# FFN operands loaded in place, loads of the output projection in another order, one operand made on VectorE

## The chip, the cores and the metric

The kernel runs on one core of a Trainium2 chip. The metric is the device time of one execution in microseconds; before the change it is 3053.76 us, the median of three runs (3052.32 to 3055.01).

## The reference

One layer of a streaming encoder works on 2048 prompt frames and 64 frames of a running stream, 2112 rows of 1024 values. An RMSNorm and an input projection feed two groups of heads: four retention heads (decaying state, group norm, gate) and eight heads of softmax attention with a forget bias. Their outputs stand side by side as `mix`, 1024 columns. What matters here comes after that:

```python
mix = concatenate([ret_output(o_r, g_r, gn_gain), o_f])
x = x + mix @ w_out
h = rmsnorm(x, g_ffn)
x = x + (silu(h @ w_gate) * (h @ w_up)) @ w_down      # width 2816
y = rmsnorm(x, norm_final_gain)
```

All of it is float32. The kernel gets float32 accuracy out of reduced-precision products by cutting every operand into a high part and a low part (`split`, L83: ScalarE copies the source rounded into the high part, VectorE writes source minus high part into the low part) and adding three products, high by high, high by low and low by high.

## The kernel before

TensorE multiplies 128x128 weights with up to 512 columns. All loads and stores are issued from one queue, SP's, in one order. The order on each engine is fixed when the program is built: a planner takes the instructions of the written program, with their costs and their data dependences, and lays them out per engine as early as its own timing allows. So instructions of a later stage can stand ahead of earlier ones where an engine would be idle. At run time nothing is reordered: an instruction that waits holds up all that stands behind it on its engine or queue.

The stages: input projection and attention projections; retention heads interleaved with the attention over the cache and then with the prompt's attention (`f_stream`); the output projection (`p3_stream`, L508); the FFN.

**Output projection.** 17 tiles of 128 rows. `load_m` (L513) brings a tile of `mix` transposed (`m`, 512 KB) and, for the prompt, the reciprocal softmax sums (`rb`, two loads of 128 KB, repeated over partitions). `halves` (L534) multiplies the attention half of `m` by `rb` (L537) and splits it into `mT`. `products` (L589) runs 24 matmuls for each of two column halves (L594); VectorE adds `x`, the residual (L633); `norm` (L544) squares and sums on ScalarE (L91), takes the root on GpSimd (L93, L95), writes the normed `h` on VectorE (L547) and stores the new `x`. `back` (L551) transposes `h` of the tile before by eight TensorE transposes (L557) in two groups that share one PSUM tile, each copied out by ScalarE (L558). It stands in the middle of the next tile's second half. After every second tile `operands` (L567) makes seven combinations of the two tiles' transposes (sums and differences for a seven-product scheme that replaces eight half-size products of the FFN), and stores them to DRAM, `h2_d` (in the trace `h_d`).

Tiles 0 to 6 run beside the prompt's attention; tile 7 and the rest need the last attention results (`f_done`), so that ten tiles run alone. The buffers `raw` of the pool `ws` are two, and `m`, `rb`, `operands`' scratch `t`, the staging of `load_h` and the first FFN weights all take turns in them.

**FFN.** Three blocks of 768, 768 and 576 rows; per block 11 pairs of 128-column stripes of the weights. `load_h` (L1032) brings a block's seven operands from `h2_d` in 14 pieces of 384 KB into staging buffers, and splits each into `hb`, one tile that holds all seven operands, high and low. For block 0 `prefetch` (L1059) does this beside the output projection, a piece at a time as tiles are done. `gu(i, s)` (L1133) runs the seven products of stripe pair `i` for the gate (s = 0) and the up projection (s = 1), 12 matmuls each (L1179); `prep` (L1087) makes and splits their weight operands four products ahead and asks for the next weights (`load_w`, L1051) when it has taken the last one; `down` (L1197) is the down projection. At a block's end L1245 to L1262 load and split the next block's operands, taking turns in two up-weight buffers (`rup`) and two down-weight buffers (`rawd`), beside the down projection; the next up weights are loaded after that (L1262).

Of the kernel before, what the change touches and what calls it, by code (L numbers as in the profile page):

```python
# [9 lines left out]
F32 = mybir.dt.float32  # L10
# [28 lines left out]
def hybrid_kernel(ctx: ExitStack, tc: tile.TileContext, a: dict):  # L39
# [468 lines left out]
    def p3_stream(last):  # L508
# [58 lines left out]
        def operands(j, b1, b2):  # L567

            w = b1.shape[2]
            lo, hi = slice(0, 4), slice(4, 8)  # L570
            t = (p3.tile([128, D], F32, tag="h", name="t", bufs=1).rearrange("p (k t) -> p k t", k=KT) if j == NT // 2 else
                 ws.tile([128, KT, 128], F32, tag="raw", name="t"))[:, :, 0:w]

            def out(n, src):
                dma(h2_d[n, :, :, j * 128:j * 128 + w], src)

            out(0, b1[:, lo])
            out(2, b1[:, hi])
            out(6, b2[:, hi])
            ve.tensor_tensor(t[:, lo], b2[:, lo], b1[:, lo], op=ALU.subtract)  # L580
            ve.tensor_tensor(t[:, hi], b2[:, hi], t[:, lo], op=ALU.subtract)
            ve.tensor_tensor(b2[:, lo], b2[:, hi], b2[:, lo], op=ALU.subtract)
            out(4, t[:, lo])
            out(1, t[:, hi])
            out(3, b2[:, lo])
            ge.tensor_tensor(b1[:, hi], t[:, hi], b1[:, hi], op=ALU.subtract)
            out(5, b1[:, hi])

# [21 lines left out]
        with tc.tile_pool(name="p3", bufs=2, reuse_waits="tile") as p3:  # L610
# [5 lines left out]
            for i in range(NT):  # L616
                while i + 1 < 16 and (i + 1) // 8 not in f_done:
                    yield None
                x = x_t.pop(i)
                if i + 1 < NT:  # L620
                    load_x(i + 1)
                    if i:
                        load_m(i + 1)
                mT = mT_t.pop(i) if i else None
                for c in range(2):
                    for q, ps in enumerate(products(mT, c) if i else early[c:c + 1]):
                        if (c, q) == (1, 1):
                            yield from back(i - 1)
                        if (c, q) == (1, 0) and 0 < i < NT - 1:
                            halves(i + 1)  # L630
                        yield 1300
                    d = slice(c * 512, (c + 1) * 512)
                    ve.tensor_tensor(x[:, d], ps, x[:, d], op=ALU.add)  # L633
# [397 lines left out]

    def load_h(n, raws):  # L1032

        hf = BLOCKS[n][1] // 2
        c0 = BLOCKS[n][0] // 2
        hb = hb_t[n] = hp.tile([128, 7, 2, 4, HALF], F32R, tag="hb", name="hb")
        raw_h = []

        def load(x):
            raw = raws()[:, 0:2 * hf].rearrange("p (k t) -> p k t", k=2)  # L1040
            j, k = divmod(x, 2)
            dma(raw, h2_d[j, :, 2 * k:2 * k + 2, c0:c0 + hf])
            raw_h.append(raw)

        yield load
        for x in range(14):
            j, k = x // 2, x % 2 * 2
            split(hb[:, j, 0, k:k + 2, 0:hf], hb[:, j, 1, k:k + 2, 0:hf], raw_h[x])
            yield None

# [8 lines left out]
    def prefetch():  # L1059

        g = load_h(0, lambda: ws.tile([128, D], F32, tag="raw", name="raw"))
        load = next(g)
        for x in range(14):
            load(x)
            next(g)
            yield 8 + x // 2 if x < 13 else 15
        load_w(0, 0, ws)
        yield 15

# [8 lines left out]
    with tc.tile_pool(name="fw", bufs=1, reuse_waits="tile") as fw, \  # L1078
# [8 lines left out]
        def prep(x):  # L1087
# [20 lines left out]
            split(o[:, 0], o[:, 1], (r0[:, lo], s2, r0[:, hi], r1[:, lo], s1, r1[:, hi], r0[:, hi])[j])  # L1108
            if j == 6 and i + 1 < NB * NP and not (s == 1 and i % NP == NP - 1):
                load_w(i + 1, s, rup if s else ws)  # L1110
# [22 lines left out]
        def gu(i, s):  # L1133

            n = i // NP
            hf = BLOCKS[n][1] // 2
            hb = hb_t[n]
            ps_t = {}
# [30 lines left out]
            for j in range(7):  # L1169
# [7 lines left out]
                for k in range(4):  # L1177
                    for m, (u, v) in enumerate(((0, 0), (0, 1), (1, 0))):
                        te.matmul(ps, w[:, u, k], hb[:, j, v, k, 0:hf], start=b == j and k == 0 and m == 0,  # L1179
                                  stop=j not in (0, 4) and k == 3 and m == 2, skip_group_check=True)  # L1180
# [44 lines left out]
        for i in range(NB * NP):  # L1225
# [13 lines left out]
            for j in gu(i, 1):  # L1239
# [3 lines left out]
                if p == NP - 1 and j in (3, 5):  # L1243
                    split_d(i, j // 4)
            if p == NP - 1 and n + 1 < NB:  # L1245
                ring = [lambda: rup.tile([128, D], F32, tag="raw", name="raw"),
                        lambda: fw.tile([128, D], F32, tag="rawd", name="rawd", bufs=2)]
                pick = [ring[x % 4 // 2] for x in range(14)]
                g = load_h(n + 1, lambda: pick.pop(0)())
                load = next(g)  # L1250
                for x in range(4):
                    load(x)
                todo = down(i)
                for x in range(14):
                    next(g)
                    if x + 4 < 14:
                        load(x + 4)
                    if x % 2 and x > 1:
                        next(todo)
                for _ in todo:  # L1260
                    pass
                load_w(i + 1, 1, rup)  # L1262
            elif p == NP - 1:
# [67 lines left out]
```

## Time and profile before

| | us |
|---|---|
| median of three runs | 3053.76 (3052.32 to 3055.01) |
| the profiled execution, its own time | 3053.89 |
| its span in the trace | 3052.1 |
| TensorE matmul busy | 2940.8 (96%) |
| VectorE busy | 1998.9 (65%) |
| ScalarE busy | 1253.6 (41%) |
| GpSimd busy | 379.4 (12%) |

The profile's second part cuts the span into 40 slices of 76 us, one digit per slice for each engine: its busy share in tenths. A row named PEclk gives the clock that TensorE was granted, in the same tenths of full speed. TensorE's busy time counts a matmul longer when the granted clock is lower, so busy time alone hides such a loss. The output projection alone on the core is at about 1437 to 1606 us of the span, the FFN's blocks begin at about 1603, 2106 and 2613 us.

### The profile page before, as it was taken

What the parts mean: (1) busy time and instruction counts of PE and PEld (TensorE: products, weight loads), DVE (VectorE), ACT (ScalarE), POOL (GpSimd) and SP (SyncE); (2) the same over time, 40 slices, a digit from 0 to 9 for tenths busy, and PEclk for the clock granted to TensorE, in tenths of its full rate; (3) what the DMA queues carried; (4) which work ended last, traced back from release to release, by engine and by line L of the source; (5) the groups of instructions that cost most, each with busy time, mean ns of one, the idle gap of its engine ahead of it and who ended that gap; (6) DMA issues with size and microseconds to landing.
All of it is one profiled execution on the core that took longest, in us unless ns stands there. A gap on an engine that the chain in (4) does not pass through costs nothing. (4 is left out here: it accounts for less than half of the span.)

```text
span 3052.1 us, 44866 instructions
## 1 busy us (share of the span) xinstructions
PE 2940.8 (96%) x16684; PEld 2644.4 (87%) x16684; DVE 1998.9 (65%) x3908; ACT 1253.6 (41%) x2642; POOL 379.4 (12%) x525
## 2 busy tenths in 40 slices
PE   8999899999999999899878999999999999999998
PEld 8999778888888888787658999998999999888887
DVE  4333554476766666765336777778777777888886
ACT  4233333265655555654223333334433333543333
POOL 0000012111111111100001101101101101211111
PEclk9999999999999999999899999999999999999999
DMA  6565533233422222544655221224522221632221
GB/s 196 173 185 174 170 110 96 88 109 89 136 76 64 80 84 86 165 140 123 196 174 168 83 69 56 84 70 131 159 70 59 83 68 58 196 97 83 84 84 59
DMA packets 438812, 341.62 MB, mean 112 GB/s; under 512 B 26954, under 2 KB 388298, under 8 KB 438594
## 3 DMA queue, kind: packets, MB, share of 16 engines
q1 hardware_dynamic: 438594, 338.76, 37.5%
q8 instruction: 131, 2.15, 0.3%
q14 instruction: 87, 0.71, 0.1%
HBM read 253.29 MB, written 85.40 MB: 111 GB/s over the span
## 5 line engine op out<-in xcount | busy, mean ns | idle before, releaser
L1179 PE MATMUL mm<-hb,w 128*128 128x384 f32 (+1 forms) x5544 | 905.6, 324 | 21.8 <-DVE G L1152 13.9
L1179 PEld LDWEIGHTS mm<-hb,w 128*128 128x128 f32 x5544 | 895.3, 189 | 31.2 <-issue 13.1
L1208 PE MATMUL dn<-wd,act 128*128 128x512 f32 (+1 forms) x2244 | 518.3, 390 | 3.1 <-ACT wd L85 3.1
L1208 PEld LDWEIGHTS dn<-wd,act 128*128 128x128 f32 (+1 forms) x2244 | 413.4, 185 | 96.2 <-ACT wd L85 3.3
L492 PE MATMUL mm<-w,hT 128*128 128x512 f32 x1632 | 445.7, 408 | 0.7 <-DVE hT L86 0.5
L1209 DVE TENSOR_TENSOR y<-y,dn 128x512 f32<-128x512 f32 (+1 forms) x374 | 254.8, 685 | 163.3 <-PE dn L1208 163.1
L86 DVE TENSOR_TENSOR w<-raw,w 128x512 fp32r<-128x512 f32 (+1 forms) x358 | 313.2, 888 | 52.2 <-ACT w L85 46.2
L492 PEld LDWEIGHTS mm<-w,hT 128*128 128x128 f32 x1632 | 291.4, 190 | 56.3 <-issue 2.2
L85 ACT CAST w<-raw 128x512 fp32r<-128x512 f32 (+1 forms) x358 | 220.9, 643 | 218.6 <-PE mm L1179 123.2
L232 PE MATMUL mm<-w,hT 128*128 128x386 f32 x1632 | 299.2, 342 | 0.9 <-ACT hT L85 0.9
L232 PEld LDWEIGHTS mm<-w,hT 128*128 128x128 f32 x1632 | 289.2, 190 | 1.6 <-ACT hT L85 1.4
L594 PE MATMUL mm<-w,mT 128*128 128x512 f32 x816 | 221.1, 420 | 14.2 <-ACT mT L85 13.2
L85 ACT CAST wd<-rawd 128x512 fp32r<-128x512 f32 x132 | 75.6, 619 | 381.4 <-PE dn L1208 380.1
L899 ACT ACTIVATE P<-P,nm 128x512 f32<-128x512 f32 (+3 forms) x288 | 189.6, 661 | 90.0 <-DVE nm L893 89.6
L85 ACT CAST hi<-t 128x512 fp32r<-128x512 f32 (+1 forms) x288 | 154.8, 562 | 138.7 <-PE t L916 135.0
L86 DVE TENSOR_TENSOR lo<-t,hi 128x512 fp32r<-128x512 f32 (+1 forms) x288 | 183.0, 656 | 37.9 <-ACT hi L85 36.2
L594 PEld LDWEIGHTS mm<-w,mT 128*128 128x128 f32 x816 | 157.8, 201 | 53.2 <-ACT mT L85 17.5
L1099 POOL TENSOR_TENSOR s<-raw 128x512 f32<-128x512 f32 x33 | 68.6, 2079 | 1058.2 <-DVE w L86 1023.8
L916 PE MATMUL t<-ident,P 128*128 128x128 f32 x1088 | 159.9, 276 | 9.1 <-DVE lo L86 5.5
L932 PE MATMUL pv<-hi,V 128*128 128x256 f32 x576 | 153.4, 292 | 1.6 <-DVE o L941 0.8
L916 PEld LDWEIGHTS t<-ident,P 128*128 128x128 f32 x1088 | 128.0, 142 | 30.2 <-DVE lo L86 10.0
L882 DVE TENSOR_SCALAR_CACHE_REDUCE P<-s 128x512 f32<-128x512 f32 x192 | 129.6, 684 | 30.6 <-PE s L879 26.2
(228 smaller groups left out, 3655.6 us busy)
## 6 DMA issues: line engine op xcount, KB each, us to landing
raw<-w_gate SPq DMA_DIRECT2D x66, 512.0 KB
raw<-w_up SPq DMA_DIRECT2D x66, 512.0 KB
rawd<-w_down SPq DMA_DIRECT2D x66, 512.0 KB
hf<-hT_d SPq DMA_DIRECT2D x34, 512.0 KB
qk_d<-qkT SPq DMA_DIRECT2D x32, 512.0 KB
h_d<-hT SPq DMA_DIRECT2D x40, 256.0 KB
KA<-qk_d SPq DMA_DIRECT2D x72, 128.0 KB
V<-v_d SPq DMA_DIRECT2D x36, 256.0 KB
```

Source lines behind the costliest of these rows:

```text
L85: se.copy(hi, src)
L86: ve.tensor_tensor(lo, src, f32(hi), op=ALU.subtract)
L232: te.matmul(ps, hT[:, u, k], w[:, v, k], start=n == 0, stop=n == 23)
L492: te.matmul(ps, hT[:, u, k], w[:, v, k], start=k == 0 and j == 0, stop=k == 7 and j == 2)
L594: te.matmul(ps, mT[:, u, k], mix_w[4 + c][:, v, k], start=k == 0 and j == 0, stop=k == 7 and j == 2)
L882: ve.tensor_scalar(o, ps, 1.0, None, op0=ALU.mult, op1=ALU.min, accum_out=m)
L899: se.activation(v, v, AF.Exp, bias=nm, scale=-1.0, accum_out=sum_t[h, u // 4][:, i % 8, ch:ch + 1])
L916: te.transpose(tr[:, c * 128:(c + 1) * 128], P_t[n, e, j // 2][:, k * 128:(k + 1) * 128], ident)
L932: te.matmul(o, V, hi[:, p], start=j == 0 and c == 0, stop=False)
L1179: te.matmul(ps, w[:, u, k], hb[:, j, v, k, 0:hf], start=b == j and k == 0 and m == 0, stop=j not in (0, 4) and k == 3 and m == 2, skip_gro ...
L1208: te.matmul(ps, act_t[i][e][:, u, f:f + m], w[c][:, v, e], start=e == 0 and j == 0, stop=e == 1 and j == 2)
L1209: ve.tensor_tensor(y[:, d], y[:, d], ps, op=ALU.add)
```

## The change

Three edits. First, the seven FFN operands are seven tiles `hb0` to `hb6` in place of one, and each is loaded by one transfer straight into the place of its low part; the split then reads that place and overwrites it. The staging buffers drop out. At a block's end the load of operand j is written behind product j of the block's last up projection, the splits stand beside the down projection, and the next up weights are loaded where they are in every other stripe pair. Second, in the output projection `load_m` of the tile after next is written right behind `halves`, and `load_x` in the middle of a tile's first half. `operands`' scratch `t` takes the buffer of `h` for every pair, where before only the last did. Third, the seventh operand is made on VectorE in a tile of its own, `t4`. The first gate weights are asked for when tile 16 is done, before it was tile 15.

```diff
@@ operands
-            t = (p3.tile([128, D], F32, tag="h", name="t", bufs=1).rearrange("p (k t) -> p k t", k=KT) if j == NT // 2 else
-                 ws.tile([128, KT, 128], F32, tag="raw", name="t"))[:, :, 0:w]
+            t = p3.tile([128, D], F32, tag="h", name="t", bufs=1).rearrange("p (k t) -> p k t", k=KT)[:, :, 0:w]
...
-            ge.tensor_tensor(b1[:, hi], t[:, hi], b1[:, hi], op=ALU.subtract)
-            out(5, b1[:, hi])
+            t4 = p3.tile([128, 4, 128], F32, tag="t4", name="t4", bufs=1)[:, :, 0:w]
+            ve.tensor_tensor(t4, t[:, hi], b1[:, hi], op=ALU.subtract)
+            out(5, t4)
 @@ p3_stream
                 x = x_t.pop(i)
-                if i + 1 < NT:
-                    load_x(i + 1)
-                    if i:
-                        load_m(i + 1)
+                if i and i + 1 < NT and i + 1 not in m_t:
+                    load_m(i + 1)
                 mT = mT_t.pop(i) if i else None
                 for c in range(2):
                     for q, ps in enumerate(products(mT, c) if i else early[c:c + 1]):
                         if (c, q) == (1, 1):
                             yield from back(i - 1)
+                        if (c, q) == (0, 2 if i else 0) and i + 1 < NT:
+                            load_x(i + 1)
                         if (c, q) == (1, 0) and 0 < i < NT - 1:
                             halves(i + 1)
+                            if i + 2 == 16 or i + 2 < 16 and (i + 2) // 8 in f_done:
+                                load_m(i + 2)
                         yield 1300
 @@ load_h
+    def load_h(n, j):
+        hf = BLOCKS[n][1] // 2
+        c0 = BLOCKS[n][0] // 2
+        hb = hb_t[n, j] = hp.tile([128, 2, 4, HALF], F32R, tag=f"hb{j}", name="hb")
+        dma(hb[:, 1, :, 0:hf], h2_d[j, :, :, c0:c0 + hf])
+
+    def split_h(n, j):
+        hf = BLOCKS[n][1] // 2
+        hb = hb_t[n, j]
+        for k in (0, 2):
+            split(hb[:, 0, k:k + 2, 0:hf], hb[:, 1, k:k + 2, 0:hf], f32(hb[:, 1, k:k + 2, 0:hf]))
 @@ prefetch
-        for x in range(14):
-            load(x)
-            next(g)
-            yield 8 + x // 2 if x < 13 else 15
+        for j in range(7):
+            load_h(0, j)
+            yield 7 + j
+            split_h(0, j)
+        yield 16
         load_w(0, 0, ws)
-        yield 15
+        yield 99
 @@ prep
-            if j == 6 and i + 1 < NB * NP and not (s == 1 and i % NP == NP - 1):
+            if j == 6 and i + 1 < NB * NP:
                 load_w(i + 1, s, rup if s else ws)
 @@ the loop over stripe pairs
             for j in gu(i, 1):
...
+                if p == NP - 1 and n + 1 < NB:
+                    load_h(n + 1, j)
             if p == NP - 1 and n + 1 < NB:
-                ring = [lambda: rup.tile([128, D], F32, tag="raw", name="raw"),
-                        lambda: fw.tile([128, D], F32, tag="rawd", name="rawd", bufs=2)]
...
-                load_w(i + 1, 1, rup)
+                split_h(n + 1, 0)
+                for j, _ in enumerate(down(i), 1):
+                    split_h(n + 1, j)
```

## Rows read from the trace of the kernel before

**Rows 1.** Part 1 of the page: busy time, share of the span, instructions.

```profile
PE 2940.8 (96%) x16684; PEld 2644.4 (87%) x16684; DVE 1998.9 (65%) x3908; ACT 1253.6 (41%) x2642; POOL 379.4 (12%) x525
```

**Rows 2.** Stretches of the span by engine, with granted clock and DMA share.

```profile
core 0: us, PE busy (x) PEld busy (x) DVE busy (x) ACT busy (x) POOL busy (x), PEclk, DMA share, GB/s
1290.00:1436.70 146.70, 141.09 (x818) 120.62 (x818) 93.91 (x209) 80.17 (x184) 10.49 (x17) 0.98 0.48 132
1436.70:1605.80 169.10, 136.42 (x555) 104.93 (x554) 65.80 (x85) 45.01 (x73) 16.56 (x26) 0.90 0.61 185
1602.80:1632.80 30.00, 19.98 (x89) 17.97 (x88) 16.98 (x27) 11.81 (x20) 6.80 (x7) 0.84 0.99 288
...
2130.00:2170.00 40.00, 33.66 (x188) 32.41 (x187) 36.58 (x54) 20.00 (x39) 14.67 (x14) 0.99 0.89 284
...
2636.00:2680.00 44.00, 37.79 (x240) 35.58 (x239) 38.12 (x62) 21.81 (x45) 15.46 (x15) 0.92 0.78 245
```

**Rows 3.** Waits of TensorE from 1436.7 to 1605.8: total us, times, longest.

```profile
PE rt L557 <- ACT hT L558: 12.5, 4, 4.5
PE mm L594 <- ACT mT L85: 11.9, 7, 3.3
```

**Rows 4.** Timeline: the norm's last step of tiles 6 and 16 (start, us, instruction).

```profile
1436.67 1.29 DVE L547 SCALAR_TENSOR_TENSOR h<-x,r,gffn 128x1024 f32<-128x1024 f32 x1 [1.10 <-POOL r L95]
...
1605.84 1.29 DVE L547 SCALAR_TENSOR_TENSOR h<-x,r,gffn 128x1024 f32<-128x1024 f32 x1 [1.09 <-POOL r L95]
```

**Rows 5.** Timeline: a tile whose sums came late, and `m` of the next.

```profile
1453.92 1.30 SPq L48 DMA_DIRECT2D rb<-rsum_d  x2
...
1462.24 0.69 DVE L537 TENSOR_TENSOR m<-m,rb 128x512 f32<-128x512 f32 x1 [3.47 <-DMA rb<-rsum_d]
...
1463.49 0.58 ACT L558 COPY hT<-rt 128x512 f32<-128x512 f32 x1
...
1464.12 0.66 PE L557 MATMUL rt<-ident,h 128*128 128x128 f32 x4 [1.94 <-ACT hT L558]
...
1464.34 0.38 SPq L48 DMA_DIRECT2D m<-mix_d  x1
...
1468.11 0.62 ACT L85 CAST mT<-m 128x512 fp32r<-128x512 f32 x1 [2.71 <-DMA m<-mix_d]
```

**Rows 6.** Timeline: a tile without a wait of TensorE.

```profile
1493.96 0.60 PE L557 MATMUL rt<-ident,h 128*128 128x128 f32 x4
...
1495.33 0.61 PE L557 MATMUL rt<-ident,h 128*128 128x128 f32 x4
...
1500.94 1.06 ACT L91 ACTIVATE h<-x 128x1024 f32<-128x1024 f32 x1 [2.15 <-issue]
...
1503.02 1.28 DVE L547 SCALAR_TENSOR_TENSOR h<-x,r,gffn 128x1024 f32<-128x1024 f32 x1 [2.17 <-POOL r L95]
...
1506.03 0.60 PE L557 MATMUL rt<-ident,h 128*128 128x128 f32 x4
```

**Rows 7.** Groups of instructions, 1436.7 to 1605.8: busy, mean ns, idle before.

```profile
L86 DVE TENSOR_TENSOR hb<-raw,hb 128x768 fp32r<-128x768 f32 x14 | 13.3, 953 | 11.3 <-ACT hb L85 11.3
...
L586 POOL TENSOR_TENSOR hT<-t,hT 128x512 f32<-128x512 f32 x5 | 8.3, 1662 | 44.3 <-DVE t L581 44.3
```

**Rows 8.** A wait of SP's queue, 1436.7 to 1605.8: total us, times, longest.

```profile
SPq L48 <- DVE mT L86: 16.3, 5, 7.4
```

**Rows 9.** Timeline at the FFN's entry: first products, what waited for weights.

```profile
1602.84 0.51 PE L1179 MATMUL mm<-hb,w 128*128 128x384 f32 x2
...
1611.74 0.62 ACT L85 CAST w<-raw 128x512 fp32r<-128x512 f32 x1 [1.46 <-DMA raw<-w_gate]
...
1624.01 1.31 POOL L1099 TENSOR_TENSOR s<-raw 128x512 f32<-128x512 f32 x1 [10.53 <-DMA raw<-w_up]
```

**Rows 10.** Timeline: first block change, the up weights' load and a late product.

```profile
2124.70 1.24 SPq L48 DMA_DIRECT2D raw<-w_up  x2
...
2169.59 2.90 PE L1179 MATMUL mm<-hb,w 128*128 128x384 f32 x8 [3.44 <-DVE G L1152]
```

More of the change, by code (lines that the diff above doesn't have):

```diff
@@ L1030, in hybrid_kernel @@
     hb_t, raw_t, w_t, sum_t = {}, {}, {}, {}
-    def load_h(n, raws):
+    def load_h(n, j):
         hf = BLOCKS[n][1] // 2
         c0 = BLOCKS[n][0] // 2
[L1036 to L1045, printed above, removed]
-        for x in range(14):
-            j, k = x // 2, x % 2 * 2
-            split(hb[:, j, 0, k:k + 2, 0:hf], hb[:, j, 1, k:k + 2, 0:hf], raw_h[x])
-            yield None
+        hb = hb_t[n, j] = hp.tile([128, 2, 4, HALF], F32R, tag=f"hb{j}", name="hb")
[5 more added lines that the diff above has]
+            split(hb[:, 0, k:k + 2, 0:hf], hb[:, 1, k:k + 2, 0:hf], f32(hb[:, 1, k:k + 2, 0:hf]))
     def load_w(i, s, pool):
@@ L1059, in prefetch @@
     def prefetch():
-        g = load_h(0, lambda: ws.tile([128, D], F32, tag="raw", name="raw"))
-        load = next(g)
-        for x in range(14):
-            load(x)
-            next(g)
-            yield 8 + x // 2 if x < 13 else 15
+        for j in range(7):
[3 more added lines that the diff above has]
+        yield 16
         load_w(0, 0, ws)
-        yield 15
+        yield 99
     pre = prefetch()
@@ L1136, in gu @@
             hf = BLOCKS[n][1] // 2
-            hb = hb_t[n]
             ps_t = {}
@@ L1178, in gu @@
                     for m, (u, v) in enumerate(((0, 0), (0, 1), (1, 0))):
-                        te.matmul(ps, w[:, u, k], hb[:, j, v, k, 0:hf], start=b == j and k == 0 and m == 0,
+                        te.matmul(ps, w[:, u, k], hb_t[n, j][:, v, k, 0:hf], start=b == j and k == 0 and m == 0,
                                   stop=j not in (0, 4) and k == 3 and m == 2, skip_group_check=True)
@@ L1244, in hybrid_kernel @@
                     split_d(i, j // 4)
+                if p == NP - 1 and n + 1 < NB:
+                    load_h(n + 1, j)
             if p == NP - 1 and n + 1 < NB:
-                ring = [lambda: rup.tile([128, D], F32, tag="raw", name="raw"),
-                        lambda: fw.tile([128, D], F32, tag="rawd", name="rawd", bufs=2)]
[L1248 to L1261, printed above, removed]
-                load_w(i + 1, 1, rup)
+                split_h(n + 1, 0)
+                for j, _ in enumerate(down(i), 1):
+                    split_h(n + 1, j)
             elif p == NP - 1:
```

## The prediction

> **What bounds the kernel now.** I read the engines' busy shares first. TensorE is busy for 96% of the span, VectorE for 65% [rows 1], so nothing off TensorE's path can pay much. 96% leaves 111 us in which it does no matmul, and the table by stretches says where to look. In 1436.7 to 1605.8, the output projection alone, TensorE is busy for 136.4 of 169.1 us, and its granted clock is 0.90 of full [rows 2]: the worst long stretch of the kernel. At the FFN's entry it loses 10 of 30 us, at the two block changes 6.3 and 6.2 us [rows 2].
>
> Next I read the waits of that first stretch. The two largest are transposes that wait for ScalarE's copy of the group before (12.5 us) and products that wait for ScalarE's cast of `mT` (11.9 us) [rows 3]. The timeline tells why ScalarE is late. The sums `rb` are asked for at 1453.9; the multiply that needs them starts at 1462.2, 8.3 us later, after a wait for that load. ScalarE's cast of `mT` stands behind the multiply and the copy of the transposes behind the cast, so the copy runs at 1463.5, and the second transposes start after 1.9 us of idle TensorE [rows 5]. The next `m` is asked for at 1464.34 and used at 1468.11, 3.8 us later, again after a wait [rows 5]. So these are loads asked for too late, because their two staging buffers are passed around `m`, `rb`, `t` and the pieces of `hb`.
>
> The norm's last step runs at 1436.67 for tile 6 and at 1605.84 for tile 16: ten tiles in 169.2 us, 16.9 us each [rows 4]. A tile without a wait, from transposes to transposes, took 1506.03 - 1493.96 = 12.07 us [rows 6]. That is what the stage could run at.
>
> **The change part by part.** *Loads of the output projection.* The loads of a tile move from the start of the tile before to the middle of the one before that. They then stand about one tile (12 us) ahead of their use, against 8.3 us that `rb` took and 3.8 us for `m` [rows 5]; both are covered. The two buffers belong to `m` and `rb` alone, since `t` and the pieces of `hb` have gone elsewhere. ScalarE no longer blocks on a piece of `hb`: its split stands a tile behind its load. SP issues about the same work: per tile `m`, two `rb`, `x` in and out, and the stores, and 7 loads in place of 14. The bytes are the same, in less time: a DMA share of 0.61 over 169.1 us [rows 2] becomes 0.61 x 169.1 / 132 = 0.78, below the 0.99 of the entry [rows 2].
>
> *The seventh operand.* Five pairs of the stretch give up a GpSimd subtract of 1.66 us [rows 7] and take one on VectorE. One of that shape takes 0.69 us [rows 5]: 5 x 0.69 = 3.5 us. VectorE then has 65.8 + 3.5 = 69.3 us of work [rows 2] in 132 us, so it is covered. Without cover it costs those 3.5 us.
>
> *`t` in `h`'s buffer.* This adds a wait. In the tile after a pair's second one, the next `h` (first written by ScalarE's square) must wait until the two stores out of `t` have landed; behind that square on ScalarE stand the next casts, and TensorE's next transposes wait for `h`. From rows: the second transposes start 1.4 us after the first [rows 6], take 0.6, the copy 0.6 [rows 5], the subtract 0.7, with 0.4 of hand-overs: the last store is issued at 3.7 us. From the square's start to the end of `h` are 1504.30 - 1500.94 = 3.4 us [rows 6], 0.2 more to the transposes. With L from the issue of the store to its landing, such a tile takes 3.7 + L + 3.4 + 0.2 = 7.3 + L, if that is over 12.07. No store's landing is in the rows. The nearest loads are 3.8 us (`m`, twice the bytes) and 8.3 us (`rb`) [rows 5]; with the first it is 11.1, no cost; with the second 15.6, or 3.5 us for each of five tiles, 18 us. I take the first, the plain transfer that a store resembles. The Trainium skill ("DMA: Bandwidth & Descriptors", section "Anatomy of one DMA — SWDGE (gpsimd) path") fits a GpSimd-issued transfer as 2.0 us and the bytes at 436 GB/s, and warns that a write to HBM completes late. By that formula 256 KB would be 2.6 us, an estimate from that page for another issue path: the tile would take 9.9 us, and the sum would stay as it is.
>
> The sum for this stage: ten tiles of 12.07 are 120.7 us. I add 1.1 us a tile, about half of the 1.9 us that a good tile still waited [rows 5], since the planner's order is made anew and need not fit: 132 us. Gain 169.2 - 132 = 37 us; bounds 48 (no wait left) and 19 (the 18 us above). Tiles 1 to 6, beside the attention, have 146.7 - 141.1 = 5.6 us idle [rows 2], shared by two streams: 0, bounds 4 either way.
>
> *The FFN's entry.* The FFN's first products run at 1602.84, but ScalarE's cast of the second gate tile waits for its load until 1611.74 [rows 9]; `t` held its buffer. It now comes early, even though it is written later, if the planner pulls it forward as it did other FFN work. But up weights can't be loaded before the projection's memory is free, and GpSimd waited 10.5 us for them until 1624.0 [rows 9]. Most of the gate's gain only moves the stall there. I take 2 us, bounds 5 (half of the 10.0 idle [rows 2]) and -7 (both gate tiles behind the last stores: asked for near 1614, used 3.8 us later, against a cast at 1611.7 [rows 9], and the first products late as well).
>
> *The block changes.* The same splits remain, two per operand, 14 x 0.95 us on VectorE [rows 7]. What goes is the late load of the next up weights: they were asked for at 2124.70, and a product still waited 3.4 us for its gate at 2169.59 behind that chain [rows 10]. They now are asked for before the down projection. TensorE's idle time there is 6.3 and 6.2 us [rows 2]. VectorE is the next limit: it is idle for only 40 - 36.6 = 3.4 and 44 - 38.1 = 5.9 us of those stretches [rows 2], and its work doesn't shrink. I take 4 us each, 8 in all; bounds 15 (all idle, and the clock of 0.92 in the second) and -3 (each load now waits for its product, and SP with it).
>
> The sum: -37 - 0 - 2 - 8 = -47 us on the profiled execution's 3053.9 us, 0.1 above the median: **3007 us**. About 0.2% (6 us) is the least that a measurement of this kernel tells from no change.
>
> **The rivals.** (a) *The buffer of `h` becomes the wait.* For it: the square must wait for two stores while the DMA share is higher than now. Against: 4.7 us of landing fit without cost. At 8.3 us the stage gains 19 in place of 37: 3053.9 - 19 - 10 = 3025 us.
>
> (b) *The FFN's part turns.* The gate tiles come behind all stores, and the block changes gain nothing because VectorE has 92% and 87% of those stretches filled [rows 2]: 3053.9 - 37 + 7 + 0 = 3024 us. Against it: the planner pulled FFN products ahead of the last tile's transposes before, the first at 1602.84 [rows 9], ahead of the last norm at 1605.84 [rows 4].
>
> (c) *The loads weren't the limit.* The reordering only uncovers another wait in the same place, say VectorE's order, and the stage keeps its 16.9 us: 3053.9 - 10 = 3044 us. Against it: the tile of 12.07 us [rows 6].
>
> (d) *Slower.* SP's queue blocks on the early `m`. Its load, now written ahead of the stores of `t`, waits at the queue's head until VectorE has split the tile before; SP waited for that split 16.3 us in five times already, 7.4 at the longest [rows 8]. The stores of `t` behind it go late, then the square, `h` and the transposes. L above then holds that wait too. A pair of tiles takes 12.07 + 7.3 + L against 2 x 16.9 = 33.8 now, so the stage loses from L = 14.4 us on, the whole kernel from 16.4 (10 us over five pairs more). At the longest wait and the longest landing together, 7.4 + 8.3 = 15.7 us, the stage loses 6; with that wait met twice, at `m` and at `rb`, 23.1 us, it loses 5 x 8.7 = 43, and the kernel ends at 3053.9 + 43 - 10 = 3087 us. Against it: the split is done in the middle of the tile, before the transposes. The Trainium skill, same page and section, says that a wait for a semaphore happens on the issuing sequencer before dispatch, so all behind waits; the trace agrees, as those 16.3 us are waits of the queue itself [rows 8].
>
> **How the numbers follow.** Forecast 60%, its own range 2990 to 3019: the bounds of the block changes and the entry, and 37 give or take 10. (a) 18%, (b) 10%, (c) 7%, (d) 5%. The range of 2988 to 3036 takes in forecast, (a) and (b) and leaves out (c), (d) and the far end of the bounds, 3053.9 - 48 - 4 - 5 - 15 = 2982. Faster holds the first three and most of (c): 0.92; the rest of (c), where the 10 us of the FFN fail too, is no change: 0.03; slower, (d): 0.05.
>
> **What would show it.** Right: ten norms (L547) about 13 us apart between tile 6 and 16, no wait for `rb` at L537, granted clock above 0.95 in that stage; the up weights' load before the first block's end, and less than 3 us idle at each block change. Wrong: ScalarE's square (L91) waiting for a store of `t` and transposes for `h`; first gate weights asked for behind the last stores of the projection; a stage that keeps 16 us a tile.

## The result and the profile after

The changed kernel takes 3028.15 us (median of four runs, 3026.82 to 3030.81), against 3054.07 for the kernel before on the same chip: a ratio of 0.9916, interval 0.990 to 0.9932. It is faster by 26 us; 47 were forecast. The profiled execution has a span of 3025.0 us against 3052.1, so 27.1 us have to be found.

Part 1 of the page of the kernel after answers to [rows 1]: TensorE's busy time fell by 17.8 us with the same 16684 matmuls, so they took less time each. In the ten tiles the granted clock went from 0.90 [rows 2] to 0.97 (table below).

```profile
PE 2923.0 (97%) x16684; PEld 2632.3 (87%) x16684; DVE 1993.5 (66%) x3917; ACT 1252.1 (41%) x2642; POOL 367.4 (12%) x516
```

The norm's last step of tiles 6 and 16, as in [rows 4], from the timeline after:

```profile
1447.15 1.29 DVE L547 SCALAR_TENSOR_TENSOR h<-x,r,gffn 128x1024 f32<-128x1024 f32 x1 [0.71 <-POOL r L95]
...
1582.24 1.28 DVE L547 SCALAR_TENSOR_TENSOR h<-x,r,gffn 128x1024 f32<-128x1024 f32 x1 [3.06 <-POOL r L95]
```

Ten tiles took 135.1 us in place of 169.2. But tile 6 comes 10.5 us later. The next two answers show whether that is a loss. They are the table by stretches, first before, then after: from tile 0's norm to the attention's last reciprocal, from there to tile 6's norm, and after also the ten tiles and the FFN's entry. Besides the columns of [rows 2], look at the numbers of matmuls in brackets.

```profile
1292.90:1413.60 120.70, 115.09 (x675) 98.40 (x674) 77.79 (x180) 68.24 (x162) 6.61 (x10) 0.99 0.49 133
1413.60:1436.70 23.10, 23.10 (x136) 19.77 (x135) 13.71 (x23) 9.90 (x19) 3.15 (x5) 1.00 0.37 111
```

```profile
1291.20:1419.40 128.20, 117.36 (x676) 100.23 (x675) 78.70 (x181) 67.59 (x161) 3.07 (x9) 0.97 0.46 129
1419.40:1447.10 27.70, 27.70 (x156) 23.51 (x155) 16.73 (x27) 12.12 (x22) 1.89 (x4) 1.00 0.47 148
1447.10:1582.20 135.10, 119.71 (x540) 95.25 (x538) 64.46 (x87) 43.01 (x70) 8.96 (x22) 0.97 0.75 227
1580.00:1610.00 30.00, 19.23 (x80) 17.62 (x81) 14.19 (x24) 11.19 (x19) 4.53 (x5) 0.73 0.78 237
```

Between the attention's end and tile 6's norm stand 20 more matmuls, without a gap of TensorE: products of tile 7 that were moved ahead of that norm. They are 27.7 - 23.1 = 4.6 us of work that the ten tiles no longer hold. What is lost is the rest: the attention ends at 1419.4 in place of 1413.6, with the same number of matmuls, 5.8 us later. Counted from tile 0's norm, which comes 1.7 us earlier, it is 128.2 in place of 120.7 us: 5.2 us more idle time of TensorE (10.8 against 5.6) and 2.3 us longer matmuls at a clock of 0.97 in place of 0.99. From the attention's end to tile 16's norm, where both kernels hold the same work but for four FFN matmuls, the time went from 192.2 to 162.8 us. So the account is: beside the attention +5.8, the projection after it -29.4, tile 16 to the end of the span (1446.3 to 1442.8) -3.5; together -27.1.

In the table of runs the first column of times is the attention's end, the second runs from there to tile 16's norm, the third from tile 16 to the span's end. The kernels ran in four batches, each beside runs of the kernel before, whose medians were 3054.07, 3057.12 (e1 to e4), 3060.54 (e5 to e8) and 3058.50 (e9 to e12): chips differ by up to 0.2%, some 3 us of the first column and of the third, so smaller differences between batches say nothing.

| kernel | ratio to before, interval | attention ends | to tile 16 | to the end |
|---|---|---|---|---|
| before | 1 | 1413.6 | 192.2 | 1446.3 |
| after | 0.9916 [0.9900, 0.9932] | 1419.4 | 162.8 | 1442.8 |
| e1: before + FFN edit | 0.9904 [0.9889, 0.9919] | 1413.3 | 164.9 | 1445.7 |
| e2: after, old load order | 0.9921 [0.9906, 0.9935] | 1423.5 | 160.8 | 1445.7 |
| e3: after, new order from tile 7 | 0.9919 [0.9905, 0.9934] | 1424.8 | 163.8 | 1446.3 |
| e4: after, `rb` in its own buffer | 0.9897 [0.9880, 0.9913] | 1418.9 | 161.0 | 1443.9 |
| e5: after, `t` back in staging | 0.9915 [0.9900, 0.9930] | 1425.9 | 161.5 | 1446.4 |
| e6: after, operand on GpSimd | 0.9906 [0.9888, 0.9924] | 1421.5 | 162.3 | 1443.6 |
| e7: after, multiply on GpSimd | 0.9864 [0.9849, 0.9878] | 1411.0 | 163.0 | 1447.2 |
| e8: after, final norms spread | 0.9932 [0.9915, 0.9948] | 1422.9 | 162.8 | 1452.1 |
| e9: e1 + load order | 0.9924 [0.9910, 0.9937] | 1420.8 | 163.3 | 1449.5 |
| e10: e1 + operand on VectorE | 0.9895 [0.9882, 0.9909] | 1416.3 | 165.5 | 1442.5 |
| e11: e1 + multiply on GpSimd | 0.9919 [0.9906, 0.9933] | 1417.0 | 170.7 | 1448.1 |
| e12: e7 + e4 | 0.9928 [0.9916, 0.9940] | 1423.7 | 165.5 | 1446.9 |

### The profile page after: what moved, and what is told of

It reads as the page before. It is cut to its first block, busy times and chain, and to the rows that moved or that the text cites. A ratio compares the mean times of both kernels' runs of the same rounds, so it can differ in the third digit from the quotient of the medians.

```text
span 3025.0 us, 44817 instructions
## 1 busy us (share of the span) xinstructions
PE 2923.0 (97%) x16684; PEld 2632.3 (87%) x16684; DVE 1993.5 (66%) x3917; ACT 1252.1 (41%) x2642; POOL 367.4 (12%) x516
## 5 line engine op out<-in xcount | busy, mean ns | idle before, releaser
L1173 PEld LDWEIGHTS mm<-hb,w 128*128 128x128 f32 x5544 | 891.5, 188 | 27.3 <-issue 14.9
L1203 DVE TENSOR_TENSOR y<-y,dn 128x512 f32<-128x512 f32 (+1 forms) x374 | 255.1, 685 | 160.8 <-PE dn L1202 160.5
L86 DVE TENSOR_TENSOR w<-raw,w 128x512 fp32r<-128x512 f32 (+1 forms) x358 | 306.1, 869 | 55.2 <-ACT w L85 49.1
L85 ACT CAST hi<-t 128x512 fp32r<-128x512 f32 (+1 forms) x288 | 154.6, 562 | 144.4 <-PE t L918 140.9
L594 PE MATMUL mm<-w,mT 128*128 128x512 f32 x816 | 210.2, 407 | 3.9 <-DVE x L635 2.1
L86 DVE TENSOR_TENSOR lo<-t,hi 128x512 fp32r<-128x512 f32 (+1 forms) x288 | 182.9, 656 | 40.8 <-ACT hi L85 38.9
L918 PE MATMUL t<-ident,P 128*128 128x128 f32 x1088 | 160.1, 276 | 17.6 <-DVE lo L86 12.4
L918 PEld LDWEIGHTS t<-ident,P 128*128 128x128 f32 x1088 | 128.4, 142 | 38.8 <-DVE lo L86 14.7
```

The lines of the kernel that those rows point to most:

```text
L85: se.copy(hi, src)
L86: ve.tensor_tensor(lo, src, f32(hi), op=ALU.subtract)
L594: te.matmul(ps, mT[:, u, k], mix_w[4 + c][:, v, k], start=k == 0 and j == 0, stop=k == 7 and j == 2)
L918: te.transpose(tr[:, c * 128:(c + 1) * 128], P_t[n, e, j // 2][:, k * 128:(k + 1) * 128], ident)
L1173: te.matmul(ps, w[:, u, k], hb_t[n, j][:, v, k, 0:hf], start=b == j and k == 0 and m == 0, stop=j not in (0, 4) and k == 3 and m == 2, ski ...
L1203: ve.tensor_tensor(y[:, d], y[:, d], ps, op=ALU.add)
```

## The experiments

The expectations below were written before I had counted the matmuls, so they take tile 6's norm as the mark of the loss; the count of moved products came after the last run. I give that mark too, and judge by the table. Letters of theories: A, the load order costs beside the attention; B, the stores of `t` do; C, VectorE is held at L537 by a late `rb`; E, the final norms' GpSimd steps hold up the weights at a block change; F, the order of VectorE's instructions decides.

**e1, the FFN edit alone.** Operands in place and the new block change; loads, `t`, seventh operand and gate weights as before.

```diff
@@ e1 against the kernel before: prefetch (load_h, split_h and the block change as in the change)
-        g = load_h(0, lambda: ws.tile([128, D], F32, tag="raw", name="raw"))
...
-        for x in range(14):
-            load(x)
...
+        for j in range(7):
+            load_h(0, j)
+            yield 7 + j
+            split_h(0, j)
```

> The kernel before with the FFN edit alone: operands loaded in place, block changes as changed; the output projection's load order, the scratch t and the seventh operand on GpSimd are those of before. Theory A (the order of the projection's loads holds VectorE at L537 beside the attention, and costs the 10.5 us by which tile 6's norm came later; the same order gives most of the 34 us of the ten tiles alone): tile 6's norm at 1437 again, ten tiles in about 155 us (only the pieces of hb are gone from the staging buffers), FFN 3 us less: about 3037 us. Rival B (the scratch t in h's buffer costs the 10.5 us, freed staging buffers give the 34): tile 6's norm at 1437, ten tiles in 140 us: about 3021 us.

It reaches the whole change's time. The projection gains 27.3 of the 29.4 us, and the attention ends at 1413.3 as before. Tile 6 comes at 1436.40, as both theories had it; the ten tiles take 141.8 us, near B's 140 and far from A's 155. Groups of TensorE's instructions in the ten tiles, before, in e1 and after (count, busy, mean ns, idle before them and its cause):

```profile
L594 PE MATMUL mm<-w,mT 128*128 128x512 f32 x468 | 129.1, 432 | 12.9 <-ACT mT L85 11.9 <-DVE mT L86 0.8
L557 PE MATMUL rt<-ident,h 128*128 128x128 f32 x80 | 14.1, 303 | 18.4 <-ACT hT L558 12.5 <-DVE h L547 5.8
```

```profile
L594 PE MATMUL mm<-w,mT 128*128 128x512 f32 x468 | 118.3, 406 | 1.7 <-ACT mT L85 1.6
L557 PE MATMUL rt<-ident,h 128*128 128x128 f32 x80 | 13.1, 287 | 13.0 <-ACT hT L558 11.6 <-DVE h L547 1.4
```

```profile
L594 PE MATMUL mm<-w,mT 128*128 128x512 f32 x448 | 112.1, 405 | 2.1 <-DVE x L635 2.1
L557 PE MATMUL rt<-ident,h 128*128 128x128 f32 x80 | 13.6, 296 | 10.3 <-DVE h L547 8.5 <-ACT hT L558 1.8
```

From before to e1 the counts are equal: 12.9 - 1.7 = 11.2 us less idle ahead of the products, 5.4 less ahead of the transposes, and 10.8 + 1.0 us less busy time, since a product takes 406 ns in place of 432. So over a third of the gain is the clock: 0.90 in these tiles before [rows 2], 0.98 in e1. One thing that stood behind the gaps is ScalarE's waits for the operands' loads, before and in e1:

```profile
ACT hb L85 <- DMA raw<-h_d: 22.7, 13, 4.9
```

```profile
ACT hb L85 <- DMA hb<-h_d: 4.8, 4, 2.9
```

Before, ScalarE stood 22.7 us in 13 waits in front of a piece of `hb`, with the casts of `mT` behind it. That this wait is the reason is argued, not shown: the casts' own waits for the multiply at L537 fell too, from 45.7 to 36.3 us, and in the kernel after, which is no slower here, the operands' waits are back:

```profile
ACT hb L85 <- DMA hb<-h_d: 16.8, 5, 7.2
```

From e1 to after, 20 products left and the idle time of the two groups went from 14.7 to 12.4 us: the other edits changed what TensorE waits for more than how long.

**e2 and e3, the load order.** All of the change but the old order; and the new order only once the attention is over.

```diff
@@ e2: p3_stream
-                if i and i + 1 < NT and i + 1 not in m_t:
-                    load_m(i + 1)
+                if i + 1 < NT:
+                    load_x(i + 1)
+                    if i:
+                        load_m(i + 1)
...
-                        if (c, q) == (0, 2 if i else 0) and i + 1 < NT:
-                            load_x(i + 1)
...
-                            if i + 2 == 16 or i + 2 < 16 and (i + 2) // 8 in f_done:
-                                load_m(i + 2)
```

```diff
@@ e3: p3_stream
+                if i + 1 < NT and i < 7:
+                    load_x(i + 1)
...
-                        if (c, q) == (0, 2 if i else 0) and i + 1 < NT:
+                        if (c, q) == (0, 2) and 7 <= i < NT - 1:
...
-                            if i + 2 == 16 or i + 2 < 16 and (i + 2) // 8 in f_done:
+                            if i >= 7 and i + 2 <= 16:
```

> The changed kernel with the order of the projection's loads of before (x and m of the next tile at the tile's start). Theory A: the 10.5 us come back, tile 6's norm at 1437, and the ten tiles lose part of their gain, some 150 us in place of 135: about 3032 us. Rival B: tile 6's norm stays at 1447, ten tiles at 140 us: about 3033 us. The place of tile 6's norm tells them apart, not the total.

> The changed kernel with the new load order only from tile 7 on, where the attention is over. Theory A: tile 6's norm at 1437 and ten tiles in 135 us: about 3018 us. Rival B: tile 6's norm at 1447: about 3028 us, as changed.

Both kept the late attention (tile 6 at 1451.21 and 1452.50), so A in its plain form fell. And the projection without the new order is no slower, 160.8 against 162.8 us: the edit on which the prediction set most of its gain gives nothing there.

**e5 and e6, `t` and the seventh operand.** Each undone alone.

```diff
@@ e5: operands
-            t = p3.tile([128, D], F32, tag="h", name="t", bufs=1)...
+            t = (p3.tile([128, D], F32, tag="h", ...) if j == NT // 2 else ws.tile([128, KT, 128], F32, tag="raw", name="t"))...
```

```diff
@@ e6: operands
-            t4 = p3.tile([128, 4, 128], F32, tag="t4", name="t4", bufs=1)[:, :, 0:w]
-            ve.tensor_tensor(t4, t[:, hi], b1[:, hi], op=ALU.subtract)
-            out(5, t4)
+            ge.tensor_tensor(b1[:, hi], t[:, hi], b1[:, hi], op=ALU.subtract)
+            out(5, b1[:, hi])
```

> The changed kernel with the scratch t back in the staging buffers. Run 2 showed that the load order is not what costs the time beside the attention. Theory C (with t out of the staging buffers the planner counts rb as ready earlier and puts its multiply, L537, ahead of attention work on VectorE, which then waits for the real load): tile 6's norm back at 1437, ten tiles at about 140 us: about 3020 us. Rival D (the seventh operand on VectorE costs it): tile 6's norm stays near 1447, about 3030 us.

> The changed kernel with the seventh operand back on GpSimd. Theory C: tile 6's norm stays near 1447, ten tiles 135 us or up to 2 us more: 3028 to 3030 us. Rival D: tile 6's norm at 1437: about 3018 us.

Tile 6 at 1451.47 and 1449.00, the projection 161.5 and 162.3: neither alone is the loss, and neither is a gain. B fell: where `t` lies makes no difference to the stage. C's own forecast for e5, tile 6 back at 1437, missed as well.

**e4 and e7, the wait at L537.** `rb` gets 2 KB a partition of its own; or the multiply goes to GpSimd, where nothing of the attention stands behind it, though the norms' root (L93, L95) does.

```diff
@@ e4: load_m
-                rb = ws.tile([128, KT, 128], F32, tag="raw", name="rb")[:, 0:4]
+                rb = p3.tile([128, 4, 128], F32, tag="rb", name="rb", bufs=1) if i else ws.tile(...)[:, 0:4]
```

```diff
@@ e7: halves
-                ve.tensor_tensor(m[:, 4:8], m[:, 4:8], rb_t.pop(i), op=ALU.mult)
+                ge.tensor_tensor(m[:, 4:8], m[:, 4:8], rb_t.pop(i), op=ALU.mult)
```

> The changed kernel with the sums rb in a buffer of their own, so that their load needs no split of the tile before. Theory A, if the late rb is the buffer's: no wait at L537, tile 6's norm at 1437, ten tiles in 130 us: about 3013 us; if rb is late because it stands behind x on SP's queue: as changed, 3028 us. Rival B: tile 6's norm at 1447, ten tiles in 130 us: about 3023 us.

> The changed kernel with the multiply by rb (L537) on GpSimd, so that its wait for rb holds GpSimd's order and not VectorE's. Theory C: the 10 us beside the attention come back, tile 6's norm near 1437; the ten tiles alone stay at 133 to 136 us although the multiply takes 1.7 us in place of 0.7: about 3018 us. Rival D: tile 6's norm stays at 1447 and the total at 3028 us or more.

The place that C names is seen in the timeline after:

```profile
1370.23 1.28 SPq L48 DMA_DIRECT2D rb<-rsum_d  x2
...
1377.84 0.69 DVE L537 TENSOR_TENSOR m<-m,rb 128x512 f32<-128x512 f32 x1 [3.85 <-DMA rb<-rsum_d]
...
1378.63 0.72 ACT L901 ACTIVATE P<-P,nm 128x512 f32<-128x512 f32 x1 [7.35 <-DVE nm L895]
...
1383.03 1.12 PE L918 MATMUL t<-ident,P 128*128 128x128 f32 x4 [3.79 <-DVE lo L86]
```

VectorE stands 3.85 us at the multiply. Behind it is the attention's row minimum (L895), which ScalarE's exponential waits for, and in the end TensorE's transposes wait 3.79 us for VectorE. e7 came out as C had it, with a total of 3019.13 us. This wait is gone there: the attention ends at 1411.0, tile 6 at 1438.51, and it is the fastest kernel of all, 0.9864. Its interval lies below that of the whole change and of e1. With its own buffer alone (e4) `rb` was still late, 16.8 us of waits and 7.6 more for `m`, and the attention ended at 1418.9 as in the kernel after.

**e9 and e10, one part more than e1.** e9 adds the new load order to e1, e10 the operand on VectorE.

```diff
@@ e9: p3_stream, on e1
-                if i + 1 < NT:
-                    load_x(i + 1)
-                    if i:
-                        load_m(i + 1)
+                if i and i + 1 < NT and i + 1 not in m_t:
+                    load_m(i + 1)
...
+                            if i + 2 == 16 or i + 2 < 16 and (i + 2) // 8 in f_done:
+                                load_m(i + 2)
```

```diff
@@ e10: operands, on e1
-            ge.tensor_tensor(b1[:, hi], t[:, hi], b1[:, hi], op=ALU.subtract)
-            out(5, b1[:, hi])
+            t4 = p3.tile([128, 4, 128], F32, tag="t4", name="t4", bufs=1)[:, :, 0:w]
+            ve.tensor_tensor(t4, t[:, hi], b1[:, hi], op=ALU.subtract)
+            out(5, t4)
```

> The kernel before with the FFN edit and the new load order alone: the scratch t stays in the staging pool, the seventh operand on GpSimd. Theory F (the order of the instructions on VectorE is what costs beside the attention: this edit alone already makes the build put the multiply L537 of a tile right behind the tile's first residual add, ahead of attention work, as in the kernel after): tile 6's norm at 1447 to 1452 us as in the kernel after, though t and the operand are as before, VectorE's waits for rb at L537 from 1290 us to that norm about 15 us against 6.6 in the run with the FFN edit alone. Rival (three small costs that add up, a third each): tile 6 at about 1440, waits for rb about 9 us. Ten tiles 133 to 138 us by both.

> The kernel before with the FFN edit and the seventh operand on VectorE alone; old load order, t in the staging pool. Theory F: the order of VectorE's instructions beside the attention is that of the FFN edit alone, so tile 6's norm stays at 1436 +- 3 us, and the ten tiles at 142 +- 3 us, total within 4 us of the FFN edit alone (ratio about 0.990). Rival (VectorE's extra 0.7 us per pair is a part of the loss): tile 6 at 1440 or later.

Waits from tile 0's norm to tile 6's, in e1, e9, e10 and after: VectorE's at L537, and TensorE's for VectorE.

```profile
DVE m L537 <- DMA rb<-rsum_d: 6.6, 3, 2.6
DVE m L537 <- DMA V<-v_d: 5.3, 1, 5.3
DVE m L537 <- DMA x_d<-x: 3.5, 1, 3.5
PE t L916 <- DVE lo L86: 3.6, 3, 2.1
PE pv L933 <- DVE lo L86: 2.4, 1, 2.4
```

```profile
DVE m L537 <- DMA rb<-rsum_d: 23.2, 6, 6.6
DVE m L537 <- issue: 4.6, 1, 4.6
PE t L918 <- DVE lo L86: 7.6, 5, 3.6
PE t L918 <- DVE P L884: 3.1, 1, 3.1
```

```profile
DVE m L537 <- DMA rb<-rsum_d: 10.9, 5, 3.2
```

```profile
DVE m L537 <- DMA rb<-rsum_d: 17.5, 6, 4.2
DVE m L537 <- issue: 4.7, 1, 4.7
PE t L918 <- DVE lo L86: 8.8, 5, 3.8
PE t L918 <- DVE P L884: 2.0, 1, 2.0
```

The profile puts a wait down to what came last, so the waits at L537 are compared whole: 15.4 us in e1 (14.7 before), 16.5 in e10, 22.2 after, 27.8 in e9. All of TensorE's waits for VectorE are 6.6 us in e1 (5.6 before), 6.8 in e10, 10.8 after, 10.7 in e9.

e9 takes the whole loss with one edit: tile 6 at 1447.55, attention's end at 1420.8, `rb` waits of 23.2 us (15 were expected). F holds there, and a sum of three small costs doesn't. e10 stayed in the old order, with 807 matmuls between the norms of tile 0 and 6 as in e1 (after: 830), but its tile 6 at 1439.87 lies between the two expectations. Counted from tile 0's norm it is 146.1 us, against 144.4 in e1 and 155.9 after; up to 1.7 us may be the operand's own. So there are two orders, and the new loads alone tip the build into the second one. In the traces they differ like this: twice in the second order L537 stands right ahead of the attention's row minimum, at about 1325 and 1378 us, as in the timeline shown under e4 and e7; so it is after and in e2, e3, e5, e6, e8 and e9. Before, in e1 and in e10 it never stands there. F's own words, right behind a tile's first residual add, don't fit: that place occurs once after and never in e9. The two orders fit e2, e5 and e6: undoing one edit leaves another that tips the build. In e2, where the loads are the old ones, that is `t`, alone or with the operand; the edit on `t` alone wasn't run.

**e11 and e12, the multiply on GpSimd elsewhere.** e11 is e1 with e7's line, e12 is e7 with e4's.

```diff
@@ e11: halves, on e1; e12: the same line on e4
-                ve.tensor_tensor(m[:, 4:8], m[:, 4:8], rb_t.pop(i), op=ALU.mult)
+                ge.tensor_tensor(m[:, 4:8], m[:, 4:8], rb_t.pop(i), op=ALU.mult)
```

> The kernel before with the FFN edit, and the multiply L537 on GpSimd; all else as before. Theory F: VectorE isn't held at L537 any more, but with the old order it was held there for only 6.6 us, so tile 6's norm at 1432 to 1437, at most 4 us earlier than with the FFN edit alone; ten tiles 139 to 145; total 3022 to 3029 (ratio 0.989). Rival (the gain of the GpSimd multiply in the kernel after came from VectorE's time, not from the held wait): the gain here is as large as there, 8 to 12 us at tile 6, near 1427.

> The kernel after with the multiply L537 on GpSimd and rb in a buffer of its own. Theory F with the load as a second part: rb is asked for earlier since it waits for no m, the multiply starts on time, tile 6 at 1436 to 1439 and ten tiles 130 to 134, total 3011 to 3018 (ratio 0.984 to 0.986). Rival (once the wait is off VectorE, its length doesn't matter): as with the GpSimd multiply alone, ten tiles 135, total 3019 (ratio 0.9865).

Both missed, all theories alike: e11's total is 3034.74 and its ten tiles 147.7, e12's total 3037.92 and tile 6 at 1451.10. Waits from tile 0 to tile 6 in e7, then in e12:

```profile
ACT mT L85 <- POOL m L537: 6.3, 2, 4.5
PE t L918 <- DVE lo L86: 1.4, 1, 1.4
```

```profile
ACT mT L85 <- POOL m L537: 10.7, 2, 9.1
PE t L918 <- DVE lo L86: 12.8, 3, 4.9
```

The wait for `rb` didn't go, it passed to other instructions. One of e12's three waits of TensorE (3.7 us at 1305.5) comes behind ScalarE's cast of `mT`, which waits 9.1 us for GpSimd's multiply with the attention's casts behind it. Another comes through the norm, whose root stands behind the multiply on GpSimd:

```profile
1323.27 1.28 DVE L547 SCALAR_TENSOR_TENSOR h<-x,r,gffn 128x1024 f32<-128x1024 f32 x1 [6.67 <-POOL r L95]
1326.73 1.66 PE L918 MATMUL t<-ident,P 128*128 128x128 f32 x8 [4.19 <-DVE lo L86]
```

The third (4.9 us at 1355.95) has nothing to do with `rb`: there ScalarE's square waits 5.3 us for a store of `t`, with casts of the attention behind it. In the ten tiles of e11 the casts of `mT` waited 38.7 us for GpSimd, in e1 36.3 us for VectorE; TensorE's transposes waited 16.0 us for ScalarE's copies against 11.6, and the granted clock was 0.93 against 0.98. So e7's gain belongs to e7's order as a whole. That VectorE was held at L537 is shown; that taking the multiply off VectorE cures it in general is refuted.

**e8, the final norms at a block change.** One every second product of gate and up, in place of one behind each gate product.

```diff
-                if old:
+                if old and j % 2 == 0:
                     finish(*old.pop(0))
...
             for j in gu(i, 1):
+                if old and j % 2 == 0:
+                    finish(*old.pop(0))
...
```

> The changed kernel with the six final norms at a block change spread over gate and up products (every second product) in place of six gate products in a row. Theory E (VectorE's work, hb's splits and the final norms, bounds the block change, so an earlier load of weights gave almost nothing): the idle time of TensorE at the two changes falls from 5.6 and 8.0 us to about 2 each: about 3020 us. Rival F (the remaining idle time is the wait for the up weights' sums on GpSimd by itself): as changed, 3028 us.

The FFN's part got 9 us longer (1452.1 against 1442.8). The norms' output tiles share buffers with the down weights, so the first of these are asked for at 2131.89 and 2151.28, in the kernel after at 2128.45 and 2138.14, and TensorE is idle for 3.5 us between 2150 and 2160. The idle time at the two changes, 7.7 and 8.7 us, didn't fall to 2 each. Since the late weights are a cause of their own, E is neither shown nor refuted by this.

## Why the prediction was right and where it was wrong

The direction was right, the time inside the range of 2988 to 3036, but 9 us outside the forecast's own, 2990 to 3019. That it lies near the times of (a) and (b) is luck, since the largest loss is at a place where no rival had one. 20 us of the 47 are missing: 10.5 at tiles 1 to 6, 3 in the ten tiles, 1.5 at the entry, 5 at the block changes.

**Tiles 1 to 6 "0, bounds 4 either way": wrong, the largest miss.** I argued from TensorE's small idle time there [rows 2] and never asked what VectorE has queued behind L537. The attention ended 5.8 us later, while VectorE's waits at L537 grew from 14.7 to 22.2 us and TensorE's for VectorE from 5.6 to 10.8. The timeline of e4 and e7 shows the path at one place, and e7, where that wait is off VectorE, has the time back; e11 and e12 show that the order built around it matters as much. The other 4.6 us at tile 6 are moved work.

**Ten tiles, -37: the size nearly right, the reason half right.** Measured are -34.1, or -29.4 with the moved products counted back. The 1.1 us a tile for waits that stay were too few: (135.1 + 4.6 - 120.7) / 10 = 1.9. I had halved the 1.9 us of [rows 5] as those of a good tile, but they are of the tile whose sums came late. "ScalarE no longer blocks on a piece of `hb`" holds in e1 and only in part after: 16.8 us in place of 22.7, and TensorE's longest wait of the stage comes behind the longest of these (a store of `t`, issued at 1498.58, may have held the square between them as well):

```profile
1500.58 0.83 ACT L85 CAST hb<-hb 128x768 fp32r<-128x768 f32 x1 [7.22 <-DMA hb<-h_d]
...
1507.89 0.86 PE L557 MATMUL rt<-ident,h 128*128 128x128 f32 x4 [4.91 <-DVE h L547]
```

The loads "one tile ahead of their use" gave nothing (e2), and L537 didn't stop waiting for `rb`: 27.9 us in the ten tiles against 34.1. TensorE hardly waits for it any more: ScalarE's casts wait 9.4 us for the multiply in place of 45.7. TensorE's largest wait is now for `h`, 8.5 us.

**Rivals.** (a): its mechanism is there, and L had about the size that I took. In the ten tiles the square waits four times for a store of `t`, 10.8 us in all. The longest wait:

```profile
1529.37 0.52 SPq L48 DMA_DIRECT2D h_d<-t  x1
...
1530.66 0.64 SPq L48 DMA_DIRECT2D h_d<-t  x1
...
1533.53 1.06 ACT L91 ACTIVATE h<-x 128x1024 f32<-128x1024 f32 x1 [4.13 <-DMA h_d<-t]
```

The store at 1530.66 is of `t4` (the profile leaves the digit out), which the square doesn't need; the last one out of `t` is that at 1529.37. So L was 4.2 us where I took 3.8. It cost little: in e5, without that wait, TensorE's transposes wait 3.6 us for `h` in place of 8.5, but its products wait 7.5 us for the residual add in place of 2.1, and the projection takes 161.5 us in place of 162.8. (b) fell in its first half: the first gate weights were asked for at 1544.69 and 1556.66, ahead of the last stores. Its second half, nothing gained at the block changes, is what came. (d) fell: the queue's waits for `mT` shrank from 16.3 us [rows 8] to 4.9. (c) was right for the load order and wrong for the staging; I had put both into one step.

```profile
SPq L48 <- DVE mT L86: 4.9, 8, 1.3
```

**The entry, -2: -0.5.** As in the prediction's own doubt, the stall moved. From tile 16's norm to the first product behind it are 24.1 us, before 24.6. The up weights were asked for at 1592.59, and GpSimd summed them at 1599.92, 17.7 us behind that norm; before it was 18.2 (1624.01 [rows 9]). TensorE still lost 10.8 of 30 us (1580 to 1610 above), 4.4 of it waiting for tile 16's `h` and 4.7 for the gate's combinations:

```profile
1606.29 18.91 PE L1173 MATMUL mm<-hb,w 128*128 128x384 f32 x96 [4.74 <-DVE G L1146]
```

**The block changes, -8: -3 and not to be told from nothing.** The -3 is all that is left behind the entry. The column to the end, which holds entry and block changes, goes from 1442.5 to 1449.5 in the kernels with the edit (e8 apart), against 1446.3 without it, and the chips account for some 3 us. The table after by stretches, the stretch before each block change and the two that answer to [rows 2]:

```profile
2046.00:2106.00 60.00, 58.58 (x292) 52.20 (x291) 48.20 (x74) 26.10 (x44) 4.79 (x4) 1.00 0.35 114
2106.00:2146.00 40.00, 35.80 (x203) 34.88 (x203) 35.69 (x54) 21.22 (x41) 13.08 (x15) 1.00 0.87 283
2544.40:2610.40 66.00, 64.59 (x335) 58.28 (x334) 53.57 (x84) 26.68 (x50) 8.34 (x7) 1.00 0.33 95
2610.40:2654.40 44.00, 37.44 (x254) 35.02 (x254) 35.26 (x64) 22.49 (x47) 14.21 (x15) 1.00 0.76 245
```

TensorE's idle time is 1.4 + 4.2 and 1.4 + 6.6 us, against 6.3 and 6.2 [rows 2]; the stretches ahead had none before. Only the second change's clock rose, from 0.92 to 1.00. The step that failed is "What goes is the late load of the next up weights". That load was hardly a cause, and [rows 10] put together two pieces of work. In the timeline before, GpSimd sums the weights asked for at 2124.70 after a wait of 0.84 us for them; the product at 2169.59 is of the next pair of stripes, whose sum had waited for VectorE:

```profile
2130.37 1.65 POOL L1099 TENSOR_TENSOR s<-raw 128x512 f32<-128x512 f32 x1 [0.84 <-DMA raw<-w_up]
...
2163.88 1.66 POOL L1099 TENSOR_TENSOR s<-raw 128x512 f32<-128x512 f32 x1 [14.00 <-DVE V L1188]
```

After, the weights are asked for at 2070.67, and a product still waits:

```profile
2070.67 1.24 SPq L48 DMA_DIRECT2D raw<-w_up  x2
...
2081.78 0.83 ACT L85 CAST hb<-hb 128x768 fp32r<-128x768 f32 x1 [1.76 <-DMA hb<-h_d]
...
2083.08 1.90 PE L1202 MATMUL dn<-wd,act 128*128 128x512 f32 x7 [1.42 <-ACT act L85]
...
2103.38 2.88 POOL L1094 TENSOR_TENSOR s<-raw 128x512 f32<-128x512 f32 x1 [11.31 <-DVE w L86]
...
2113.49 2.70 PE L1173 MATMUL mm<-hb,w 128*128 128x384 f32 x14 [2.31 <-DVE G L1146]
```

The weights are asked for 32.7 us before GpSimd sums them, and what GpSimd waited for is VectorE's split (L86), not the load. That split, at 2102.60, stands right behind the last splits of the operands. The product waits for the gate's chain, as before. And ScalarE now waits for an operand's load (1.76 us) with the down projection's cast behind it, which costs TensorE 1.42 us that are new. What ends the gate's chain late is open: VectorE's work, as I said, or the final norms' steps on GpSimd.

**The signs.** Of those named for right, the norms (13.5 us apart), the clock (0.97) and the early load of the up weights came; no wait at L537 and less than 3 us idle at a block change didn't. Of those named for wrong, the square waiting for a store of `t`, with transposes waiting for `h`, came.

## What to carry to other kernels

Test freeing a shared staging buffer alone before anything is reordered: here that alone gave the whole net gain (e1). When a load or an instruction is moved earlier, list what stands behind its consumer on the consumer's engine; an earlier place with an unready operand holds all of that up. And before a landmark of two kernels is compared, count the instructions between its ends: here 4.6 of 10.5 us were work that had changed sides. Before a load and a late reader are put in one sentence, check that they are of the same piece of work: in [rows 10] they weren't.

## What was not expected of the hardware

How much of a gain can be the clock's. From the attention's end to tile 16's norm TensorE's idle time went from 32.7 to 15.4 us, and its busy time from 159.5 (689 matmuls) to 147.4 us (694): of the 29.4 us, 12.1 are matmuls that took less time, with the granted clock at 0.91 before and 0.98 after. The prediction has no term for this; it came in unnamed with the tile of 12.07 us [rows 6], in which TensorE was busy throughout and the clock stood at 1.00.
